# Low parts of weights by transfers that add, and Strassen's products for 14 FFN pairs of the first layer

## The chip, the cores and the metric

The kernel runs on one core of a Trainium2 chip. A core has five engines that work side by side, each through its own queue in order: TensorE (PE: matmuls; PEld is its weight loads), VectorE (DVE), ScalarE (ACT), GpSimd (POOL) and SyncE (SP, which here only issues DMA transfers). Sixteen DMA engines move data between memory and the on-chip buffer, and inside that buffer. The metric is the device time of one execution in microseconds (us).

## The reference

Two layers over 512 tokens of width 1024, in float32, then a final norm:

```
mod = c @ w_ada + b_ada                 # 6 vectors of 1024 per layer: shifts, scales, gates
h = rms_norm(x) * (1 + sc_m) + sh_m
x_lru, q_down, kv_down, k_rope, gate_a, gate_b = split(h @ w_in)
y_a = rg_lru(conv(x_lru))               # a gated linear recurrence
y_b = mla(q_down, kv_down, k_rope)      # 8 heads, causal
y = sigmoid(gate_a) * y_a + sigmoid(gate_b) * y_b
x = x + g_m * (y @ w_out)
h = rms_norm(x) * (1 + sc_f) + sh_f
gate, up = split(h @ w_ffn_in)          # 2 x 2816 columns: 22 tiles each of 128
x = x + g_f * ((silu(gate) * up) @ w_ffn_out)
```

## The kernel before

Activations lie with channels on the 128 partitions and the 512 tokens along the row, so a product with a weight of 1024 x 128 is 8 steps of 128 channels. To keep float32's precision at the speed of the shorter format fp32r, each operand is split in a high part (rounded to fp32r) and a low part (what is left), and each step is three matmuls: high x high, high x low, low x high (`mm3`). A product of 1024 x 128 with 512 tokens is thus 24 matmuls of 512 columns; it is called a unit here.

Weights come by `w_cols`: a transfer of 512 KB into one of 3 buffers `raw`, a high part `whi` by ScalarE, and a low part `wlo`, raw - whi, by VectorE (`split`), each in one of 3 buffers. For the FFN output of layer 1 alone the low part is made in another way: ScalarE writes -whi, and a transfer issued by GpSimd adds raw to it in place (`accum_op`). Such a transfer is called a transfer that adds. A raw buffer is free again when its low part is done.

A layer has an attention part (input products `w_in`: the inputs of the recurrence, the downward projections and 16 gates; then heads, recurrence, merging), a projection of 8 units (`w_out`), and the FFN. The FFN runs over 22 pairs (gate and up tile); products with the FFN output weights (`fo_block`) are done in three blocks of pairs (`FCUTS`: pairs 0 to 6, 7 to 13, 14 to 21), the first two beside the next block's pairs, the last one alone. The first pair is computed ahead of the norm (`Ahead`). Of the others the first `NPLAIN[l]` are plain: two units of 24 matmuls each. The rest are done by `fi_pair`, with Strassen's scheme in Winograd's form: gate and up tile, halves of the channels and halves of the tokens are the 2 x 2 blocks, and 7 products of 4 steps x 3 matmuls of 256 columns, 84 in all, take the place of 48 of 512. It needs sums of weight blocks (`w_quarters`: 4 sums and 5 further splits on VectorE and ScalarE) and of token halves (`token_halves`, once per layer). Layer 0 has no such pair (21 plain ones and the one ahead), layer 1 has 16.

The modulation vectors are made by VectorE: a transfer of 512 KB into one of 2 buffers `graw`, and one reduction of 128 x 1024 against c (`mod_column`, shown as CUSTOM_DVE_ANT_0 in the profile and as ISA in the order of instructions). Those of layer 1 are steps of a background list (`bg`): one step is recorded after each unit, and the rest when the list is drained.

No engine's order is written by hand. All operations are recorded with what they need; `Recorder.order` then plans a run with assumed durations, and each engine takes, at each moment of the plan, the ready operation that has the longest chain behind it. What comes out is a fixed order for each engine. The plan's figures for a transfer issued by GpSimd are `POOL_DMA` (its time on GpSimd's queue) and `POOL_LAT` (what follows until it has landed); the plan lets SyncE's transfers share one rate, and does not count GpSimd's against it. All recorded operations are issued in one line (L524 before, L530 after), so rows are told apart by the tiles that they name.

## Time and profile before

| | |
|---|---|
| time, median of 3 runs | 1330.85 us (1329.75 to 1331.48) |
| profiled execution | 1330.39 us, its span 1328.6 us |
| TensorE busy | 99% of the span |
| VectorE, ScalarE, GpSimd busy | 71%, 51%, 18% |
| granted TensorE clock, mean | 0.998 of full speed |
| DMA | 186.44 MB, mean 140 GB/s |

The span runs from the first to the last instruction of the profiled execution; its time is 1.8 us longer. Matmuls are pipelined, so what one of them costs is read from the step between the starts of two, not from its own duration. The span has layer 0's first products (to 58 us), its attention part (to 272), projection and change to the FFN (to 328), FFN (to 682); then layer 1's attention part (to 916), projection (to 977), FFN and end.

### The profile page before, as it was taken

The page shows a single profiled execution, that of the slowest core. Times are in us where ns is not written, and L with a number is a line of the kernel's source. Part 1 is how long each engine was busy: PE and PEld are TensorE (multiplying, and loading weights), DVE is VectorE, ACT ScalarE, POOL GpSimd, SP SyncE. Part 2 cuts the span into 40 slices and gives each one's busy share as a digit, 9 for nine tenths or more (in the row PEclk, how much of TensorE's full clock was granted, in tenths as well). Part 3 has the DMA queues.
Part 4 walks back from the last instruction along what each step waited for, and adds up shares of the span by engine and source line. Part 5 has one row for each costly group of instructions (what it writes and reads, how often), then busy time and mean ns, then how long its engine had stood idle before and what let it go on. Part 6 is the DMA issues. An engine that isn't in the chain of part 4 may idle for free.

```text
span 1328.6 us, 18151 instructions
## 1 busy us (share of the span) xinstructions
PE 1309.8 (99%) x6788; PEld 1119.4 (84%) x6788; DVE 945.7 (71%) x1625; ACT 676.2 (51%) x1057; POOL 235.1 (18%) x250
## 2 busy tenths in 40 slices
PE   9999999999999999999999999999999999999997
PEld 7787878888888888888888888888888999899986
DVE  7999887897755555555679886666687766667634
ACT  4597676635322222222356867855474544444532
POOL 0414534314000000000211433312400000000011
PEclk9999999999999999999999999999999999999999
DMA  8744344172655555555414231211333444544473
GB/s 291 237 121 152 117 127 143 64 229 104 220 177 181 172 209 176 183 206 172 147 59 149 94 115 64 96 48 48 106 101 109 133 118 135 155 129 134 126 157 109
DMA packets 56012, 186.44 MB, mean 140 GB/s; under 512 B 7026, under 2 KB 7282, under 8 KB 55924
## 3 DMA queue, kind: packets, MB, share of 16 engines
q1 hardware_dynamic: 52468, 173.75, 39.6%
q0 software_dynamic: 3456, 11.54, 4.7%
q8 instruction: 53, 0.87, 0.3%
q14 instruction: 35, 0.29, 0.1%
HBM read 167.44 MB, written 2.10 MB: 128 GB/s over the span
## 4 chain that ended last, share of the span: by engine, by line
PE 88%; DMA 4%; ACT 3%; DVE 2%; SPq 1%; issue 1%; POOL 0%; DVEq 0%; ACTq 0%
PE mm L524 78%; PE s L524 4%; PE o L524 2%; PE pt L524 2%; DMA raw<-in_w_in_dram 1%; DMA raw<-in_w_ada_dram 1%; SPq L524 1%; DMA graw<-in_w_ada_dram 1%; ACT whi L524 1%; ACT L524 0%; DMA raw<-in_w_ffn_in_dram 0%; DVE raw L524 0%; DMA raw<-in_w_first_dram 0%; DMA crow<-in_c_dram 0%; ACT xc L524 0%
## 5 line engine op out<-in xcount | busy, mean ns | idle before, releaser
L524 ACT ACTIVATE whi<-raw 128x1024 fp32r<-128x1024 f32 (+2 forms) x192 | 199.3, 1038 | 434.6 <-PE mm L524 318.1
L524 DVE TENSOR_TENSOR wlo<-raw,whi 128x1024 fp32r<-128x1024 f32 (+1 forms) x167 | 206.9, 1240 | 103.9 <-ACT whi L524 99.9
L524 PE MATMUL mm<-hl,whi 128*128 128x512 f32 x432 | 168.9, 391 | 0.3 <-DVE hl L524 0.3
L524 PE MATMUL mm<-hh,whi 128*128 128x512 f32 x432 | 166.2, 394 | 1.8 <-ACT ri L524 1.4
L524 PE MATMUL mm<-hh,wlo 128*128 128x512 f32 x416 | 161.8, 390 | 0.0
L524 PE MATMUL mm<-al,whi 128*128 128x512 f32 (+1 forms) x360 | 139.1, 386 | 0.0
L524 PE MATMUL mm<-ah,whi 128*128 128x512 f32 (+1 forms) x360 | 138.9, 386 | 0.0
L524 PE MATMUL mm<-ah,wlo 128*128 128x512 f32 (+1 forms) x360 | 138.5, 385 | 0.0
L524 PE MATMUL mm<-fh,whi 128*128 128x512 f32 x336 | 130.5, 389 | 0.0
L524 PE MATMUL mm<-fh,wlo 128*128 128x512 f32 x336 | 130.5, 389 | 0.0
L524 PE MATMUL mm<-fl,whi 128*128 128x512 f32 x336 | 130.4, 389 | 0.0
L524 PEld LDWEIGHTS mm<-hh,whi 128*128 128x128 f32 x432 | 80.9, 188 | 19.0 <-ACT ri L524 1.5
L524 PEld LDWEIGHTS mm<-hl,whi 128*128 128x128 f32 x432 | 81.2, 188 | 17.4 <-DVE hl L524 1.4
L524 PEld LDWEIGHTS mm<-hh,wlo 128*128 128x128 f32 x416 | 78.1, 188 | 16.0
L524 PE MATMUL mm<-xqh,wsl 128*128 128x256 f32 x320 | 90.4, 283 | 0.0
L524 PE MATMUL mm<-xql,wsh 128*128 128x256 f32 x320 | 90.4, 283 | 0.0
L524 PE MATMUL mm<-xqh,wsh 128*128 128x256 f32 x320 | 90.4, 284 | 0.0
L524 DVE CUSTOM_DVE_ANT_0 graw<-graw,cb,cols 128x1024 f32<-128x1024 f32 x64 | 83.4, 1303 | 6.5 <-DMA graw<-in_w_ada_dram 5.7
L524 POOL TENSOR_SCALAR wsa<-raw,mod 128x128 f32<-128x128 f32 x24 | 17.2, 736 | 388.6 <-PE mm L524 339.4
L524 PEld LDWEIGHTS mm<-ah,whi 128*128 128x128 f32 x360 | 67.7, 188 | 13.2
L524 PEld LDWEIGHTS mm<-ah,wlo 128*128 128x128 f32 x360 | 67.7, 188 | 13.2
L524 PEld LDWEIGHTS mm<-al,whi 128*128 128x128 f32 x360 | 67.7, 188 | 12.6
(257 smaller groups left out, 3055.7 us busy)
## 6 DMA issues: line engine op xcount, KB each, us to landing
graw<-in_w_ada_dram SPq DMA_DIRECT2D x88, 512.0 KB, 4.5
raw<-in_w_ffn_in_dram SPq DMA_DIRECT2D x88, 512.0 KB, 3.4
raw<-in_w_in_dram SPq DMA_DIRECT2D x47, 512.0 KB, 3.4
raw<-in_w_ffn_out_dram SPq DMA_DIRECT2D x32, 448.0 KB, 3.5
raw<-in_w_out_dram SPq DMA_DIRECT2D x16, 512.0 KB, 3.4
raw<-in_w_ffn_out_dram SPq DMA_DIRECT2D x16, 512.0 KB, 3.9
wlo<-raw POOLq DMA_DIRECT2D x16, 448.0 KB, 4.4
raw<-in_w_ada_dram SPq DMA_DIRECT2D x8, 512.0 KB, 4.7
```

The costliest lines, as they stand in the source:

```text
L524: o.call(*(real(v) for v in o.a), **{k: real(v) for k, v in o.k.items()})
```

## The change

Three edits. First, the low parts of more weights are made by transfers that add: all of `w_in` that goes by `x_lru` and `gate` (20 weights in layer 0, 24 in layer 1; here GpSimd writes -whi, by `tensor_scalar`), `w_out` (16) and layer 0's `w_fo` (24; in both of these ScalarE writes -whi, as layer 1's `w_fo` did already). `w_fi` and the units of `Ahead` keep the subtraction on VectorE. Second, `NPLAIN` of layer 0 goes from 21 to 7, so 14 pairs go by `fi_pair`, and the layer takes the path with `token_halves`. Third, the plan's figures for GpSimd's transfers go from 1200 and 6000 ns to 900 and 3700.

```diff
-NPLAIN = (21, 5)
+NPLAIN = (7, 5)
...
-POOL_DMA = 1200.0
-POOL_LAT = 6000.0
+HOW_IN = "gg"
+HOW_OUT = "aa"
+HOW_FI = "vv"
+HOW_FO = "aa"
+HOW_A1 = "v"
+POOL_DMA = 900.0
+POOL_LAT = 3700.0
...
+    def split_by(how, hi, lo, src):
+        if how == "v":
+            split(hi, lo, src)
+            return
+        A.activation(hi, src, AF.Copy)
+        if how == "a":
+            A.activation(lo, f(hi), AF.Copy, scale=-1.0)
+        else:
+            G.tensor_scalar(lo, f(hi), -1.0, 1.0, ALU.mult, ALU.mult)
+        G.dma_start(f(lo), src, accum_op=ALU.add)
...
-    def w_cols(src, nk=KD, raws=None, dma=False):
+    def w_cols(src, nk=KD, raws=None, how="v"):
...
-        if dma:
-            A.activation(hi[:, : nk * P], raw[:, : nk * P], AF.Copy)
-            A.activation(lo[:, : nk * P], f(hi[:, : nk * P]), AF.Copy, scale=-1.0)
-            G.dma_start(f(lo[:, : nk * P]), raw[:, : nk * P], accum_op=ALU.add)
-        else:
-            split(hi[:, : nk * P], lo[:, : nk * P], raw[:, : nk * P])
+        split_by(how, hi[:, : nk * P], lo[:, : nk * P], raw[:, : nk * P])
...
-                ps = product(w_cols(w_in[l, n]))
+                ps = product(w_cols(w_in[l, n], how=HOW_IN[l]))
...
-            ps = product(w_cols(w_in[l, off + h]))
+            ps = product(w_cols(w_in[l, off + h], how=HOW_IN[l]))
...
-            [(m, FULL) for m in range(KD)], yh, yl, lambda m: w_cols(w_out[l, m]), done_out,
+            [(m, FULL) for m in range(KD)], yh, yl, lambda m: w_cols(w_out[l, m], how=HOW_OUT[l]), done_out,
...
-                lambda m: w_cols(w_fo[l, m, :, k0 * P : (k0 + nk) * P], nk, dma=last), done,
+                lambda m: w_cols(w_fo[l, m, :, k0 * P : (k0 + nk) * P], nk, how=HOW_FO[l]), done,
```

In numbers of instructions: 14 pairs x 48 = 672 matmuls of 512 columns go, 14 x 84 = 1176 of 256 columns come; 98 subtractions of weights on VectorE go (82 of 1024 columns, 16 of 896): the 84 whose low part is now made by a transfer, and 14 because `w_quarters` subtracts one weight where a plain pair has two; GpSimd has 108 transfers that add instead of 24, and 44 negations of 1024 columns more.

Since the plan is made anew, each engine's order changes. Three places:

GpSimd's queue where layer 0's first input products end; w16 is a chain of small operations for the recurrence's parameters, 108 and 109 (137 and 138) are the high and low part of the first (second) input weight. Before:

```order
L524 TENSOR_TENSOR w16_4_71<-w16_4_71,w16_3_561 128x16
L524 TENSOR_SCALAR w16_4_71<-w16_4_71 128x16
L524 TENSOR_TENSOR w16_4_71<-w16_4_71,w16_3_561 128x16
L524 TENSOR_SCALAR w16_4_71<-w16_4_71 128x16
L524 TENSOR_TENSOR w16_4_71<-w16_4_71,w16_3_561 128x16
L524 TENSOR_SCALAR w16_4_71<-w16_4_71 128x16
L524 TENSOR_TENSOR w16_4_71<-w16_4_71,w16_3_561 128x16
```

After:

```order
L530 TENSOR_TENSOR w16_4_71<-w16_4_71,w16_3_561 128x16
L530 TENSOR_SCALAR w16_4_71<-w16_4_71 128x16
L530 TENSOR_TENSOR w16_4_71<-w16_4_71,w16_3_561 128x16
L530 TENSOR_SCALAR w16_4_71<-w16_4_71 128x16
L530 TENSOR_SCALAR wlo_109_626<-whi_108_611 128x1024
L530 TENSOR_TENSOR w16_4_71<-w16_4_71,w16_3_561 128x16
L530 DMA wlo_109_626<-raw_107_569 128x1024
L530 TENSOR_SCALAR wlo_138_649<-whi_137_630 128x1024
L530 TENSOR_SCALAR w16_4_71<-w16_4_71 128x16
L530 DMA wlo_138_649<-raw_136_589 128x1024
```

Two negations and two transfers that add stand in the middle of the chain of small operations.

TensorE's queue at the same place; mm_45 is the last of the first products, mm_110 and mm_139 are the products with those two weights. Before:

```order
L524 MATMUL mm_45_333<-hl_37_609,whi_96_591 128x512
L524 MATMUL mm_110_679<-hh_22_271,whi_108_611 128x512
L524 MATMUL mm_110_679<-hl_30_285,whi_108_611 128x512
L524 MATMUL mm_110_679<-hh_22_271,wlo_109_622 128x512
L524 MATMUL mm_110_679<-hh_23_328,whi_108_611 128x512
```

After:

```order
L530 MATMUL mm_45_333<-hl_37_609,whi_96_591 128x512
L530 MATMUL mm_110_674<-hh_22_271,whi_108_611 128x512
L530 MATMUL mm_110_674<-hl_30_285,whi_108_611 128x512
L530 MATMUL mm_139_681<-hh_22_271,whi_137_630 128x512
L530 MATMUL mm_139_681<-hl_30_285,whi_137_630 128x512
L530 MATMUL mm_110_674<-hh_22_271,wlo_109_626 128x512
L530 MATMUL mm_110_674<-hh_23_328,whi_108_611 128x512
```

Two matmuls of the second product have moved between the high parts of the first and its first matmul with a low part.

VectorE's queue at the beginning of layer 0's last FFN block; x0_73, x1_79 are residuals after a unit, xw and sacc the low part and the sum of squares made from them, ISA with graw a reduction for layer 1's modulation. Before:

```order
L524 SCALAR_TENSOR_TENSOR x0_73<-mm_1099_5512,mod0_5_3488,x0_73 128x512
L524 ISA graw_1094_5519,mod1_5_5360<-graw_1094_5519,cb_187,cols1_130 128x1024
L524 ISA mod1_5_5360 128x1
L524 TENSOR_TENSOR wlo_1119_5568<-raw_1117_5456,whi_1118_5547 128x1024
L524 SCALAR_TENSOR_TENSOR xw_1102_5575<-x0_73,mod1_1_3759,xh_1101_5563 128x512
L524 ISA graw_1095_5549,mod1_5_5360<-graw_1095_5549,cb_187,cols1_130 128x1024
L524 ISA mod1_5_5360 128x1
L524 SCALAR_TENSOR_TENSOR x1_79<-mm_1106_5551,mod0_5_3488,x1_79 128x512
L524 TENSOR_TENSOR wlo_1126_5597<-raw_1124_5495,whi_1125_5589 128x1024
L524 TENSOR_TENSOR sacc_1100_5559<-sacc_1100_5559,sq_1107_5600 128x512
L524 SCALAR_TENSOR_TENSOR xw_1109_5614<-x1_79,mod1_1_3759,xh_1108_5604 128x512
```

After:

```order
L530 SCALAR_TENSOR_TENSOR x0_73<-mm_1333_6522,mod0_5_3691,x0_73 128x512
L530 ISA graw_1302_6529,mod1_2_5920<-graw_1302_6529,cb_187,cols1_130 128x1024
L530 ISA mod1_2_5920 128x1
L530 SCALAR_TENSOR_TENSOR xw_1336_6588<-x0_73,mod1_1_3851,xh_1335_6583 128x512
L530 ISA graw_1303_6558,mod1_2_5920<-graw_1303_6558,cb_187,cols1_130 128x1024
L530 ISA mod1_2_5920 128x1
L530 SCALAR_TENSOR_TENSOR x1_79<-mm_1340_6560,mod0_5_3691,x1_79 128x512
L530 ISA graw_1304_6580,mod1_2_5920<-graw_1304_6580,cb_187,cols1_130 128x1024
L530 ISA mod1_2_5920 128x1
L530 TENSOR_TENSOR sacc_1334_6575<-sacc_1334_6575,sq_1341_6620 128x512
L530 SCALAR_TENSOR_TENSOR xw_1343_6636<-x1_79,mod1_1_3851,xh_1342_6626 128x512
```

Subtractions of weights are gone from this queue, and reductions stand in their place; up to the first operand of layer 1 (ht) 17 of them follow the first residual, where 2 did before. In the attention part of layer 1, behind that operand, there are 10, where there were none. In the FFN before that block, 14 stand in the plain pairs and 15 in the Strassen pairs, where 54 did in all between the projection and the last block.

## Rows read from the trace of the kernel before

**Rows 1.** the page, part 1: busy us, share of the span, instructions

```profile
PE 1309.8 (99%) x6788; PEld 1119.4 (84%) x6788; DVE 945.7 (71%) x1625; ACT 676.2 (51%) x1057; POOL 235.1 (18%) x250
```

**Rows 2.** stages: length, PE, PEld, DVE, ACT, POOL busy us, clock, DMA, GB/s

```profile
58.00:272.00 214.00, 207.32 (x1051) 174.91 (x1050) 188.59 (x373) 155.16 (x272) 86.43 (x80) 1.00 0.39 125
272.00:328.00 56.00, 56.00 (x256) 46.53 (x256) 47.70 (x70) 26.21 (x37) 20.09 (x22) 1.00 0.53 174
...
682.00:916.00 234.00, 233.97 (x1184) 199.24 (x1183) 181.37 (x358) 167.34 (x281) 65.82 (x63) 1.00 0.27 84
...
1032.00:1250.00 218.00, 216.96 (x1542) 204.77 (x1541) 149.59 (x254) 105.12 (x172) 14.04 (x16) 1.00 0.48 132
...
1278.00:1308.00 30.00, 30.00 (x144) 24.81 (x143) 11.51 (x31) 11.89 (x15) 4.35 (x5) 1.00 0.67 141
```

**Rows 3.** the chain that ended last, from start time, us

```profile
327.91 351.60 PE mm L524 x1550
...
688.97 3.79 PE mm L524 x16
...
1145.38 5.77 DMA raw<-in_w_ffn_in_dram
```

**Rows 4.** timeline of TensorE: start, us, operation

```profile
1138.17 0.28 PE L524 MATMUL mm<-xqh,wsl 128*128 128x256 f32 x1
...
1140.69 0.29 PE L524 MATMUL mm<-xqh,wsl 128*128 128x256 f32 x1
...
1143.32 0.39 PE L524 MATMUL mm<-ah,whi 128*128 128x512 f32 x1
...
1149.90 0.39 PE L524 MATMUL mm<-ah,wlo 128*128 128x512 f32 x1
```

**Rows 5.** groups by line and form: busy us, mean ns of one

```profile
L524 DVE TENSOR_TENSOR wlo<-raw,whi 128x1024 fp32r<-128x1024 f32 x143 | 180.8, 1265 | 99.0 <-ACT whi L524 96.0 <-PE pt L524 0.3
...
L524 DVE CUSTOM_DVE_ANT_0 graw<-graw,cb,cols 128x1024 f32<-128x1024 f32 x64 | 83.4, 1303 | 6.5 <-DMA graw<-in_w_ada_dram 5.7 <-ACT cb L524 0.4
...
L524 ACT ACTIVATE wlo<-whi 128x1024 fp32r<-128x1024 f32 x8 | 8.5, 1058 | 0.2
...
L524 POOL DMA_DIRECT2D wlo<-raw x24 | 21.0, 875 | 322.8 <-ACT wlo L524 174.0 <-ACT pq L524 74.6 <-PE mm L524 60.2
...
L524 POOL TENSOR_SCALAR sc<-sc,sm 128x512 f32<-128x512 f32 x16 | 14.9, 929 | 73.7 <-DVE sm L524 55.5 <-PE o L524 12.7 <-issue 5.4
...
L524 POOL TENSOR_SCALAR sc<-sc,sm 128x128 f32<-128x128 f32 x16 | 11.3, 709 | 0.0
```

**Rows 6.** the tile wlo: its transfers

```profile
DMA to landing us min/median/max: 4.2/4.6/7.9
```

**Rows 7.** timeline of ScalarE at the first input weight

```profile
56.05 1.06 ACT L524 ACTIVATE whi<-raw 128x1024 fp32r<-128x1024 f32 x1 [0.71 <-DMA raw<-in_w_in_dram]
```

**Rows 8.** timeline of TensorE there

```profile
61.60 0.39 PE L524 MATMUL mm<-hh,whi 128*128 128x512 f32 x1
```

**Rows 9.** timeline of GpSimd there

```profile
58.53 0.57 POOL L524 TENSOR_SCALAR w<-w 128x16 f32<-128x16 f32 x1
```

**Rows 10.** timeline of VectorE and GpSimd at 96 us

```profile
96.37 1.57 POOL L524 TENSOR_TENSOR ri<-ri,xc 128x512 f32<-128x512 f32 x1 [7.61 <-ACT ri L524]
...
96.70 2.32 DVE L524 TENSOR_TENSOR wlo<-raw,whi 128x1024 fp32r<-128x1024 f32 x1
```

**Rows 11.** the page, parts 3 and 6: DMA queues; issues, median to landing

```profile
q1 hardware_dynamic: 52468, 173.75, 39.6%
q0 software_dynamic: 3456, 11.54, 4.7%
...
graw<-in_w_ada_dram SPq DMA_DIRECT2D x88, 512.0 KB, 4.5
```

**Rows 12.** timeline of VectorE at layer 0's last FFN block

```profile
638.30 0.75 DVE L524 SCALAR_TENSOR_TENSOR x<-mm,mod,x 128x512 f32<-128x512 f32 x1 [1.58 <-PE mm L524]
...
683.37 2.08 DVE L524 SCALAR_TENSOR_TENSOR ht<-x,mod,rs 128x512 f32<-128x512 f32 x3 [1.91 <-ACT rs L524]
```

More of the change, by code (lines that the diff above doesn't have):

```diff
@@ L887, in w_quarters @@
         h, l_ = hl_tiles()
-        split(h, l_, raws[0])
+        split_by(HOW_A1, h, l_, raws[0])
         res["A11"], res["A12"] = (h[:, lo_], l_[:, lo_]), (h[:, hi_], l_[:, hi_])
@@ L1418, in w_fi_cols @@
         def w_fi_cols(m):
-            return w_cols(w_fi[l, m // 2 + (m % 2) * NF])
+            return w_cols(w_fi[l, m // 2 + (m % 2) * NF], how=HOW_FI[l])
         def residual(m, cs, ps):
```

## The prediction

> **What bounds the kernel now.** I read the busy times first: TensorE is busy in 99% of the span, VectorE in 71%, ScalarE in 51%, GpSimd in 18% [rows 1]. Then the busy time by stage [rows 2]: only the attention part of layer 0 (58 to 272 us) leaves TensorE visibly idle, 214.00 - 207.32 = 6.7 us, and there VectorE is at 188.59 / 214 = 88%. In the same part of layer 1 VectorE is at 181.37 / 234 = 78% and TensorE is idle 0.03 us. In the FFN stages TensorE is full; with Strassen (1032 to 1250 us) VectorE is at 69% and TensorE idle about 1 us. The chain of work that ended last says the same [rows 3]: one piece of 351.60 us is TensorE alone (layer 0's FFN), and in Strassen's stage the chain leaves TensorE where a weight load comes late, 5.77 us at 1145.38. So time can come from two places: fewer or shorter matmuls, and layer 0's 6.7 us of waits behind a full VectorE.
>
> **Strassen for 14 pairs.** Where nothing waits, 29 steps of 512 columns take 1149.90 - 1143.32 = 6.58 us, 0.2269 us each, and 21 steps of 256 columns take 1140.69 - 1138.17 = 2.52 us, 0.120 us each [rows 4]. A plain pair is 2 x 8 x 3 = 48 matmuls of 512 columns, 10.89 us; a Strassen pair is 7 products of 4 x 3 = 84 matmuls of 256 columns, 10.08 us. The saving is 0.81 us a pair, **-11.3 us** for 14.
>
> The price is VectorE work. Layer 1 does the same with VectorE at 69% [rows 2], with one stall of about 1.2 us at 1153 where an FFN load came late [rows 3]. Layer 0 adds reductions for layer 1's modulation (1.303 us each [rows 5]), 15 during its Strassen pairs in the new order: some 20 us over about 217, so 79% instead of 69%. That still fits. Bounds of the stalls: 0, and one such 1.2 us per block of FFN output, 3 in all, plus as much again: 5. I take **+1.5**.
>
> **Low parts by transfers that add.** A subtraction on VectorE, 1.265 us, goes for 44 attention input weights (20 in layer 0, 24 in layer 1), 16 of the projection and 24 of layer 0's FFN output. In layer 0's attention that is 20 x 1.265 = 25 us of 188.59, so VectorE falls to about 76%, where layer 1 shows no idle TensorE at 78%. Of the 6.7 us I take **-5** (bounds 0 and -6.7): some waits are for loads, which this edit does not help.
>
> What replaces it is slower in latency. For the input weights GpSimd negates the high part: the trace has no such operation at 1024 columns; 128 columns take 0.709 us in the mean, 512 take 0.929 [rows 5], so some 1.2 by that slope, and 0.7 to 2.4 as bounds. For the projection and FFN output ScalarE does it in 1.058 us; in the projection it is busy for 26.21 of 56 us [rows 2], so 8 more are covered. Then GpSimd issues a transfer: 0.875 us on its queue [rows 5], landing 4.2 / 4.6 / 7.9 us (least, median, most) after the issue [rows 6]. So a low part is ready some 6 us after its high part instead of 1.3.
>
> Where it is not covered: the first weight of layer 0. Its high part starts at 56.05 [rows 7], and TensorE comes to it at 61.60 [rows 8], so before, 4 us lay between. In the new order its negation stands behind four polynomial steps on GpSimd, the fourth of which ends at 58.53 + 0.57 = 59.1 [rows 9]. With 1.2 for the negation, some 0.3 for the step between, and 4.6 to land, it is there at 65.2. TensorE has four matmuls with high parts first, 61.60 + 0.9 = 62.5, and then waits: **+2.8** (2.3 with the shortest landing, 6 with the longest). Later weights have other TensorE work ahead of them and the weights' buffers hold three, so I count none.
>
> A rule against this edit: GpSimd's reads and VectorE's operations with two inputs from SBUF hold each other up. The rows show it: a subtraction that takes 1.265 us in the mean took 2.32 at 96.70, beside a GpSimd operation at 96.37 [rows 10]. The Trainium skill, "SBUF — State Buffer", Who interferes with whom, says that the second to issue is blocked until the first is done; the trace agrees. My sum takes the mean durations, in which such waits are; if each of the 44 negations costs a further 1.1 us (2.32 - 1.265), that is 48 us spread over both engines, and the rival below prices it.
>
> **The transfers' own load.** Queue q1 moved 173.75 MB in 39.6% of 1328.6 us, so 512 KB (0.524 MB) take 1.59 us of all 16 engines. Queue q0, the transfers that add, took 4.7% for 11.54 MB: 2.84 us for 512 KB [rows 11]. In layer 0's attention 20 of them add 57 us to a share of 0.39 over 214 us: 0.66. That is covered. In the projection (272 to 328 us, share 0.53 [rows 2]) up to 8 add 23 us to 30 of 56: 0.94. Lateness there between 0 and 4; I take **+1**.
>
> The worst place is the end of layer 0. The reductions that Strassen pushes out of the FFN stage move into its last block: 17 stand between the first residual and layer 1's first operand where 2 stood, on the in-order queue of VectorE. In the trace these two points are 638.30 and 683.37 [rows 12]; the block itself begins one unit of 24 x 0.227 = 5.45 us earlier, so 50.5 us hold all of it. DMA work in that time: 17 reductions x 1.59 = 27, some 8.5 weight loads x 1.59 = 13.5, 5 transfers that add x 2.84 = 14: 55 us. Besides, the reductions have two buffers: each pair costs 1.30 for a reduction, 4.5 to land [rows 11] and some 0.2 between, 6.0 us, 51 us for 8.5 pairs with no queueing, and if each pair waits behind one load or transfer (2.2 on average), 70. So layer 1's operand comes 0 to 19 us late; I take 9, nearer to the DMA's own sum. TensorE reads it at 688.97 [rows 3], where it can be there at about 685: 4 us are covered. **+5** (bounds 0 and 15).
>
> Layer 1's attention loses 24 x 1.265 = 30 us of VectorE work and gets 10 reductions more, 13 us. TensorE was not idle there: **0** (bounds -1 and +5, for late low parts).
>
> Sum: -11.3 + 1.5 - 5 + 2.8 + 1 + 5 + 0 = **-6.0**. The profiled execution took 1330.39 us, so 1324.4; the median of the runs is 0.46 above it: 1324.8, which I round to **1324.5**.
>
> **The rivals.**
> *All is covered.* The DMA queues take the extra load in gaps, the last block is not late, TensorE keeps full in layer 0. For: layer 1's last block (1278 to 1308 us) runs such transfers at a DMA share of 0.67 with TensorE full [rows 2]. Then -11.3 - 6.7 + 2.8 + 1 = -14: about 1316, down to 1312 without stalls.
> *GpSimd and VectorE block each other.* Of the 48 us one in six to eight reaches TensorE, 6 to 8 us: 1331, no change that a measurement of this kernel can tell (within 0.2%, 2.7 us). For: the subtraction at 96.70. Against: GpSimd is busy for 86.43 of 214 us there, so most operations meet nothing.
> *The DMA queues bound the last block: slower.* Loads wait behind reductions on the in-order issue queue, so the block's own weights come late too. A unit needs 3 x 1.59 + 2.84 = 7.6 us of DMA against 5.45 of TensorE: 8 x 2.15 = 17 us in place of my 5: 1336.5. It turns slower than before once lateness at this place passes 11 us. For: two reductions stand in each unit. Against: three weight buffers are filled ahead.
> *The change does not do what it says.* The new order has 84 matmuls of 256 columns for each of 14 pairs; excluded.
>
> **How the numbers follow.** Forecast (1319 to 1329 with its bounds) 50%; all covered 22%; blocking 13%; DMA bound 12%; other 3%. Faster by over 0.2% (below 1328.2): most of the forecast's 50, the 22 and a little of the blocking, 0.74. Within 0.2%: 0.14. Slower: 0.12. The range leaves out the half of each outer case: 1312 to 1333.
>
> **What would show it.** The FFN stage of layer 0 shorter by about 10 us with 256-column steps of 0.120; a TensorE wait of about 3 us near 62 us; idle TensorE in the rest of layer 0's attention under 3 us; a wait near the start of layer 1 behind a reduction on VectorE that waits for its load. Wrong would be: no wait there and a time near 1316, or FFN units of the last block paced above 5.45 us and a time above 1333; also TensorE waits spread over both attention parts behind low parts in flight.

## The result and the profile after

The changed kernel takes 1376.92 us (median of 4 runs, 1374.7 to 1382.45); the kernel before took 1331.16 us beside it (4 runs). The ratio is 1.0343 [1.0311, 1.0375]: it is 46 us slower, where 6 us less were forecast. The profiled execution took 1374.7 us, its span is 1372.8 us.

The page of the changed kernel (parts 1, 3 and 6; columns as in [rows 1] and [rows 11]):

```profile
PE 1320.4 (96%) x7292; PEld 1146.9 (84%) x7292; DVE 967.0 (70%) x1747; ACT 767.9 (56%) x1207; POOL 346.4 (25%) x378
...
q1 hardware_dynamic: 52468, 173.75, 37.3%
q0 software_dynamic: 15552, 54.53, 21.3%
...
graw<-in_w_ada_dram SPq DMA_DIRECT2D x88, 512.0 KB, 4.8
...
wlo<-raw POOLq DMA_DIRECT2D x76, 512.0 KB, 5.2
```

TensorE's share fell from 99% to 96% [rows 1], and no other engine has become full: VectorE, the busiest of them, is at 70%. The transfers that add went from 4.7% to 21.3% of the DMA engines' span; 54.53 MB in 292 us is 2.81 us for 512 KB, the 2.84 us of the prediction. A reduction's load lands 4.8 us after its issue instead of 4.5.

By stage (columns as in [rows 2]; the last three rows are short stretches inside the first and the fourth):

```profile
58.00:288.30 230.30, 212.87 (x1036) 178.69 (x1035) 171.00 (x346) 168.53 (x282) 118.76 (x123) 0.96 0.62 163
288.30:337.50 49.20, 46.98 (x204) 38.58 (x203) 33.49 (x50) 23.56 (x30) 15.81 (x23) 0.97 0.80 232
...
351.30:644.00 292.70, 290.84 (x1832) 263.81 (x1831) 224.21 (x371) 141.13 (x220) 15.64 (x18) 1.00 0.57 174
644.00:705.20 61.20, 51.56 (x216) 41.85 (x215) 37.20 (x54) 25.62 (x32) 23.92 (x28) 0.92 0.89 263
...
719.00:965.00 246.00, 237.31 (x1171) 200.49 (x1171) 173.53 (x353) 170.61 (x283) 116.11 (x113) 0.98 0.59 153
...
65.30:68.20 2.90, 2.90 (x7) 2.32 (x8) 2.90 (x5) 2.81 (x5) 2.48 (x6) 0.50 0.99 192
...
697.60:703.10 5.50, 5.50 (x13) 4.39 (x14) 4.78 (x8) 2.74 (x4) 5.50 (x8) 0.50 0.77 266
703.20:705.20 2.00, 2.00 (x10) 1.64 (x9) 0.80 (x1) 0.00 (x0) 1.84 (x3) 1.00 0.90 352
```

Before, attention and projection of layer 0, its last FFN block, and the attention of layer 1:

```profile
58.00:269.90 211.90, 205.22 (x1039) 172.94 (x1038) 186.66 (x370) 155.03 (x271) 86.43 (x80) 1.00 0.38 122
269.90:315.00 45.10, 45.10 (x204) 37.55 (x203) 40.00 (x56) 18.70 (x25) 19.88 (x22) 1.00 0.61 198
...
627.70:676.10 48.40, 48.40 (x215) 40.11 (x214) 33.83 (x40) 19.70 (x26) 15.74 (x22) 1.00 0.42 137
...
688.70:920.40 231.70, 231.67 (x1171) 197.36 (x1171) 178.77 (x355) 163.52 (x276) 65.82 (x63) 1.00 0.28 87
```

Three of them now let TensorE wait where before it was idle little or not at all: layer 0's attention for 17.4 us (6.7 before [rows 2]), the last FFN block of layer 0 for 9.6 us (0 before), layer 1's attention for 8.7 us (0.03 before). VectorE has become emptier, as meant: 74% in layer 0's attention instead of 88%, 71% in layer 1's instead of 78%. And the DMA share is 0.62 and 0.59 there (0.39 and 0.27 before), 0.80 in the projection (0.61), 0.89 in the last block (0.42).

What TensorE waited for over the whole span, the first four entries (us in total, times, longest):

```profile
PE mm L530 <- DMA wlo<-raw: 14.9, 4, 7.7
PE pt L530 <- POOL sc L530: 6.1, 1, 6.1
PE s L530 <- DVE kl L530: 3.8, 1, 3.8
PE o L530 <- ACT ph L530: 3.7, 1, 3.7
```

The low parts by transfers lead the list, with 4 waits: one at the start of layer 0's attention, one in its projection, two in its last FFN block. The other entries are waits for engines that were late themselves.

The stages of all profiled executions, from the first matmul of one stage to the first of the next in TensorE's timeline. First row: us of before; then differences to it. "Attention 0" begins with the first product; that comes up to 2.9 us sooner or later from run to run, as the first loads arrive, which is the column "start".

| kernel | start | attention 0 | projection 0 | to FFN 0 | FFN 0, 21 pairs | last block | to layer 1 | attention 1 | rest | span |
|---|---|---|---|---|---|---|---|---|---|---|
| before | 17.9 | 251.9 | 45.2 | 12.7 | 299.9 | 48.5 | 12.7 | 231.7 | 408.1 | 1328.6 |
| changed | -0.8 | +19.2 | +4.1 | +1.3 | -7.5 | +12.8 | +1.2 | +14.3 | -0.4 | +44.2 |
| transfers | -0.6 | +19.4 | +2.8 | +1.5 | -0.1 | +1.7 | +0.2 | +6.6 | +0.7 | +32.3 |
| strassen | -0.1 | -0.9 | 0.0 | 0.0 | -10.5 | -0.5 | +8.2 | +8.1 | +0.2 | +4.6 |
| thin | +0.9 | +7.2 | 0.0 | +0.3 | -10.6 | +0.1 | +7.9 | +8.1 | -1.1 | +12.8 |
| thin_a | -0.5 | +5.6 | 0.0 | +0.4 | -10.8 | +0.6 | +8.6 | +3.6 | -1.4 | +6.1 |
| in_v | +1.2 | +1.2 | +4.9 | +0.9 | -6.3 | +8.9 | +1.5 | +5.4 | +1.6 | +19.3 |
| strassen_bg | -0.7 | +2.0 | 0.0 | 0.0 | -10.1 | -0.3 | 0.0 | +2.3 | -0.8 | -7.6 |
| after_bg | +1.6 | +22.6 | +4.1 | +1.5 | +4.0 | -0.5 | +0.5 | +7.7 | -0.5 | +40.8 |
| fo_bg | +2.9 | +2.1 | 0.0 | 0.0 | +2.0 | -0.5 | +0.5 | +0.7 | +0.7 | +8.2 |
| fo_bg_raw4 | -0.6 | +5.4 | 0.0 | 0.0 | -2.3 | -0.4 | 0.0 | +2.4 | -0.8 | +3.7 |
| load_only | +2.5 | +6.2 | 0.0 | 0.0 | -2.3 | -0.3 | 0.0 | +0.7 | +2.5 | +9.4 |
| after_raw4 | +2.5 | +9.7 | +6.1 | 0.0 | -6.6 | +9.9 | +2.9 | +12.8 | -0.9 | +36.4 |
| plan_old | -0.3 | +12.5 | +0.3 | +0.9 | -8.1 | +0.1 | +10.8 | +12.7 | -0.4 | +28.5 |
| after_all | +0.6 | +9.9 | +1.5 | 0.0 | -4.5 | +0.6 | 0.0 | +9.2 | -0.9 | +16.6 |

Attention 0 has differed by up to 7 us (-0.9 to +6.2) between kernels that have no new work in it (strassen, strassen_bg, fo_bg, load_only): the order is planned anew for each, so less than that is not read there. And each row is a single execution: strassen_bg's eight took 1320.97 to 1330.93 us. One execution of the kernel plan_dma took 4350.63 us, its profiled one: its profile is not used, and its time is the median of its other runs.

**Two places in the timeline.** First the wait that was forecast near 62 us (start, us, engine, operation; in brackets the idle time before and what ended it):

```profile
57.97 1.07 ACT L530 ACTIVATE whi<-raw 128x1024 fp32r<-128x1024 f32 x1 [1.88 <-DMA raw<-in_w_in_dram]
...
58.93 1.18 POOL L530 TENSOR_SCALAR wlo<-whi 128x1024 fp32r<-128x1024 f32 x1
...
60.45 1.05 POOL L530 DMA_DIRECT2D wlo<-raw  x1
...
65.22 0.79 PE L530 MATMUL mm<-hh,wlo 128*128 128x512 f32 x1 [3.06 <-DMA wlo<-raw]
```

The negation follows its high part at once, takes 1.18 us (1.2 forecast), the transfer is issued at 60.45, and TensorE waits 3.06 us for it, until 65.22 (65.2 forecast). That the time fits to 0.1 us is in part luck: the high part began 1.9 us later than before (57.97, 56.05 in [rows 7]) and so ended at 59.04, just when GpSimd's four polynomial steps, from which the forecast counted, were done as well.

Then the longest wait of all, in the last FFN block of layer 0:

```profile
676.05 1.29 DVE L530 CUSTOM_DVE_ANT_0 graw<-graw,cb,bsc 128x1024 f32<-128x1024 f32 x1 [6.18 <-DMA graw<-in_w_ada_dram]
...
677.38 2.80 SPq L530 DMA_DIRECT2D graw<-in_w_ada_dram  x2
680.28 0.37 SPq L530 DMA_DIRECT2D raw<-in_w_in_dram  x1
...
680.52 0.63 ACT L530 ACTIVATE sq<-x 128x512 f32<-128x512 f32 x1 [7.05 <-DVE x L530]
...
682.75 1.06 ACT L530 ACTIVATE wlo<-whi 128x1024 fp32r<-128x1024 f32 x1
...
685.29 2.49 POOL L530 TENSOR_SCALAR wsa<-raw,mod 128x128 f32<-128x128 f32 x4 [10.56 <-DMA raw<-in_w_in_dram]
687.76 2.99 POOL L530 TENSOR_SCALAR wsb<-raw,mod 128x128 f32<-128x128 f32 x3
690.70 0.87 POOL L530 DMA_DIRECT2D wlo<-raw  x1
...
697.53 0.80 PE L530 MATMUL mm<-ah,wlo 128*128 128x512 f32 x1 [7.69 <-DMA wlo<-raw]
```

ScalarE has written -whi of a weight at 682.75 + 1.06 = 683.81. GpSimd could issue its transfer then, but the transfer stands behind seven small operations for layer 1's first products in GpSimd's in-order queue, and the first of these has waited 10.56 us for a weight load that SyncE issued only at 680.28. So the transfer goes out at 690.70, 6.9 us late, and TensorE waits 7.69 us, until 697.53. Both ends of this go back to one late load: VectorE had stood idle for 6.18 us until 676.05, before a reduction whose load had not landed. Behind that reduction stood a residual, for which ScalarE waited 7.05 us until 680.52 before it came to this weight; and when the reduction had freed its buffer, SyncE issued two loads for reductions (677.38) and only then, in its in-order queue, the weight load at 680.28.

### The profile page after: what moved, and what is told of

It reads as the page before. It is cut to its first block, busy times and chain, and to the rows that moved or that the text cites. A ratio compares the mean times of both kernels' runs of the same rounds, so it can differ in the third digit from the quotient of the medians.

```text
span 1372.8 us, 19779 instructions
## 1 busy us (share of the span) xinstructions
PE 1320.4 (96%) x7292; PEld 1146.9 (84%) x7292; DVE 967.0 (70%) x1747; ACT 767.9 (56%) x1207; POOL 346.4 (25%) x378
## 3 DMA queue, kind: packets, MB, share of 16 engines
q0 software_dynamic: 15552, 54.53, 21.3%
## 4 chain that ended last, share of the span: by engine, by line
PE 63%; issue 12%; DMA 10%; DVE 8%; POOL 5%; ACT 1%; SPq 1%; DVEq 0%; POOLq 0%; ACTq 0%
PE mm L530 55%; DMA wlo<-raw 3%; DMA graw<-in_w_ada_dram 3%; PE s L530 3%; PE o L530 2%; PE pt L530 2%; DMA raw<-in_w_ffn_in_dram 1%; DVE graw L530 1%; POOL wlo L530 1%; DMA raw<-in_w_ffn_out_dram 1%; POOL wsa L530 1%; DVE t L530 1%; DVE xc L530 1%; SPq L530 1%; POOL sc L530 1%
## 5 line engine op out<-in xcount | busy, mean ns | idle before, releaser
L530 ACT ACTIVATE whi<-raw 128x1024 fp32r<-128x1024 f32 (+3 forms) x178 | 184.1, 1035 | 271.4 <-PE mm L530 191.5
L530 POOL DMA_DIRECT2D wlo<-raw x108 | 95.4, 886 | 690.4 <-ACT wlo L530 486.2
L530 PE MATMUL mm<-xqh,wsh 128*128 128x256 f32 x600 | 170.0, 284 | 1.6 <-DVE pq L530 1.5
L530 PE MATMUL mm<-xql,wsh 128*128 128x256 f32 x600 | 169.5, 283 | 0.0
L530 PE MATMUL mm<-xqh,whi 128*128 128x256 f32 (+1 forms) x432 | 142.8, 331 | 0.2 <-ACT pq L530 0.2
L530 PE MATMUL mm<-xqh,wlo 128*128 128x256 f32 (+1 forms) x432 | 142.3, 330 | 0.0
L530 PE MATMUL mm<-xql,whi 128*128 128x256 f32 (+1 forms) x432 | 142.0, 330 | 0.0
L530 PEld LDWEIGHTS mm<-xqh,wsh 128*128 128x128 f32 x600 | 114.6, 192 | 3.1 <-DVE pq L530 2.8
L530 PEld LDWEIGHTS mm<-xql,wsh 128*128 128x128 f32 x600 | 115.0, 192 | 0.5
L530 PEld LDWEIGHTS mm<-xqh,wsl 128*128 128x128 f32 x600 | 114.9, 192 | 0.0
```

Of the source, the lines that this page charges most:

```text
L530: o.call(*(real(v) for v in o.a), **{k: real(v) for k, v in o.k.items()})
```

## The experiments

**transfers**: the change with plain pairs, `NPLAIN = (21, 5)`.

> The change without Strassen in layer 0: its first layer's FFN goes back to 21 plain pairs, all low parts stay with the transfers that add. Against the kernel before, the changed kernel loses 18.5 us in layer 0's attention, 14.3 us in layer 1's, 5.4 us in the first projection and its change to the FFN, 14 us in the last FFN block of layer 0 and its norm, and gains 7.5 us in that FFN. Theory 1 (the transfers that add cause the losses by their load and lateness): both attention parts and the projection stay long, 18.5 + 14.3 + 5.4 = 38 us over before, the last block is a little late: 1369 to 1375 us. Theory 2 (Strassen, which pushes the modulation reductions into the last block and layer 1's attention, causes those two): layer 1's attention and the last block come back, 18.5 + 5.4 = 24 us remain: about 1355 us. Theory 3 (the transfers cost little by themselves): 1331 to 1338 us.

Measured: 1363.89 us, ratio 1.025 [1.0222, 1.0278]. The low parts by transfers, with the plan's new figures, cost 32 us by themselves: both attention parts and the projection stay long (+19.4, +6.6, +2.8), so theory 3 falls. But layer 1's attention loses only 6.6 of the 14.3 us and the last block 1.7 of 12.8: the time is 5 us below theory 1's range, and theory 2 has a share.

**strassen**: the kernel before with `NPLAIN = (7, 5)`, and nothing else.

> Strassen for 14 pairs of layer 0 alone: the kernel before with that one number changed, all other low parts by VectorE and the plan's old figures. 14 x 0.81 = 11.3 us less TensorE work. Theory 1 (the transfers cause the losses): attention parts as before, the last block may be some us late because the reductions still move into it: 1320 to 1327 us. Theory 2 (the displaced reductions cause the last block's and layer 1's losses, 28 us): about 1345 us. Theory 3 (VectorE becomes full in the Strassen pairs without the relief by transfers): the FFN does not get shorter, 1328 to 1335 us.

Measured: 1337.3 us, ratio 1.0039 [1.0025, 1.0053]. The FFN is 10.5 us shorter, as worked out, though VectorE keeps all subtractions. 16 us are lost behind it, more than theory 1 had and less than theory 2. The stages to layer 1 and of its attention in this run:

```profile
664.00:685.00 21.00, 16.26 (x66) 13.20 (x64) 16.75 (x27) 7.55 (x13) 3.57 (x3) 0.84 0.69 218
685.00:925.00 240.00, 234.72 (x1169) 199.21 (x1170) 198.14 (x377) 165.50 (x280) 70.24 (x63) 0.99 0.32 100
```

And its timeline at the end of layer 0, of VectorE and then TensorE:

```profile
667.33 1.48 DVE L524 CUSTOM_DVE_ANT_0 graw<-graw,cb,cols 128x1024 f32<-128x1024 f32 x1
...
668.74 1.27 DVE L524 CUSTOM_DVE_ANT_0 graw<-graw,cb,cols 128x1024 f32<-128x1024 f32 x1
...
669.95 0.74 DVE L524 SCALAR_TENSOR_TENSOR x<-mm,mod,x 128x512 f32<-128x512 f32 x1
...
671.74 0.68 DVE L524 TENSOR_TENSOR sacc<-sacc,sq 128x512 f32<-128x512 f32 x1
...
672.48 0.80 PE L524 MATMUL o<-ones,sacc 128*128 128x1 f32 x3 [3.61 <-DVE sacc L524]
```

VectorE runs without a gap here: the reductions have their data, but stand ahead of the residual (669.95) and of the sum of squares (671.74) that TensorE waits for 3.61 us, at 672.48. So it is VectorE's queue that is too long at this place, not DMA.

**thin**: the changed kernel in its own order, with each transfer that adds cut to 16 partitions when it is issued:

```diff
+                if o.eng == "POOL" and o.dur == POOL_DMA:
+                    args = [v[:16] for v in args]
```

> The changed kernel with the same order of every engine, but each of the 108 transfers that add moves 16 of 128 partitions (64 of 512 KB), so most of each low part stays -whi and the output is not the reference's. The issue on GpSimd's queue, the negations, the waits and the fixed part of the latency stay; the load on the DMA engines goes from 21.3% of the span to under 3%. Theory 1a (the load of the transfers delays the weights' and reductions' loads): most of the loss goes, 1320 to 1335 us. Theory 1b (the longer way of a low part through GpSimd's in-order queue and the fixed latency of a transfer): most stays, 1360 to 1372 us. Theory 2 (the reductions' place in the order): attention and last block stay late, 1355 us or more.

Measured: 1345.45 us, ratio 1.0109 [1.0074, 1.0144], 10 us above theory 1a's range. 31 us of the 46 go with the size of the transfers, though every instruction stays in its place: theory 1a for most of it. The load did not fall as far as expected. An eighth of the bytes still takes a third of the DMA engines' time, 7.3% of the span and not under 3%:

```profile
q0 software_dynamic: 3456, 6.82, 7.3%
```

The last block, the projection and 12 of 19 us of attention 0 come back; what is left, 12.8 us of span, is Strassen's pattern (+7.9 and +8.1, less what the FFN gains) and 7.2 us in attention 0. A transfer lands sooner, too. The summary for the low parts' tile in thin:

```profile
DMA to landing us min/median/max: 2.9/3.1/6.8
```

The same of the changed kernel:

```profile
DMA to landing us min/median/max: 4.2/5.0/10.9
```

so low parts are ready and raw buffers are free 2 us earlier as well, and thin doesn't part load from lateness and held buffers.

**in_v**: the change with `HOW_IN = "vv"`.

> The changed kernel with the attention input weights' low parts back on VectorE by subtraction (44 weights); the projection and FFN output keep the transfers, Strassen stays. Theory 1 (the input transfers and their negations cause both attention parts' loss, 33 us): 1344 us or less. Theory 2 (the reductions cause layer 1's part): only layer 0's 18.5 us go, about 1358 us. Theory 3 (VectorE's relief was worth something there): layer 0's attention is about as long as before the change, layer 1's is longer since VectorE has 24 subtractions and 10 reductions more: 1350 to 1360 us.

Measured: 1349.78 us, ratio 1.0145 [1.0108, 1.0181]. That is 6 us above theory 1's bound, at the lower edge of theory 3's range. Attention 0 is back within 1.2 us of before, attention 1 at +5.4: the transfers of the attention inputs, with their negations, cost 18 and 9 us there, beyond anything that VectorE's relief bought.

**strassen_bg**: strassen with the reductions recorded in the pairs, at the end of `fi_pair`:

```diff
+            bg(2)
```

> Strassen alone was 4.6 us longer in its span than before: its FFN was 10.5 us shorter, but the change to layer 1 8.2 us and layer 1's attention 8.1 us longer. Here each Strassen pair of layer 0 also records two steps of the background list, as a plain pair does, so the reductions for layer 1 stand in the FFN as before (22 between the first residuals of the first and the second block, 18 and 20 before that, 2 in the last block) and none in layer 1's attention. Theory A (the displaced reductions cause both losses): both vanish, 16 us less than Strassen alone, about 1321 us. Theory B (VectorE, 84% busy in Strassen's FFN, cannot take 24 reductions more, 31 us of 288, 95%): the losses vanish but the FFN stage gains less than 5 us instead of 10.5: 1326 to 1332 us. Theory C (the two losses have another cause, such as a new order that is poor by itself): 1337 us as before.

Measured: 1325.79 us (8 runs), ratio 0.9946 [0.9924, 0.9968]: faster than both kernels. Theory A: to layer 1 0.0, attention 1 +2.3, and the FFN keeps 10.1 of its 10.5 us. Theory B falls:

```profile
329.00:619.00 290.00, 289.84 (x1831) 263.60 (x1831) 265.74 (x435) 125.68 (x202) 0.00 (x0) 1.00 0.58 194
```

VectorE is busy for 265.74 of 290 us, 92%, and TensorE is idle for 0.16 us. So 92% of VectorE did not hold up TensorE in this stage.

**after_bg**: the changed kernel with the same line.

> The changed kernel with the same two background steps recorded in each Strassen pair. If displaced reductions and transfers add up: the last block of layer 0 comes back from 12.8 us over before to about 2, layer 1's attention from 14.3 to about 6.5, as in the run with transfers alone, and the FFN stays near 7 us shorter; layer 0's attention and projection keep their 23 us: 1355 us. If the reductions' loads and the transfers crowd the DMA queues in the FFN instead, the FFN loses its gain: 1362 us.

Measured: 1370.74 us, ratio 1.0277 [1.0255, 1.0299]. The last block (-0.5) and attention 1 (+7.7) come back as expected, but the FFN goes from -7.5 to +4.0: the second outcome in kind, though 9 us above its 1362. With the transfers, the FFN loses its gain when the reductions are put back (DMA share 0.68 there, 0.57 in the change).

**thin_a**: thin, with `HOW_IN = "aa"` (ScalarE negates).

> The kernel with thin transfers (16 of 128 partitions, so the output is not the reference's) once more, but ScalarE instead of GpSimd writes -whi of the attention input weights (the order is planned anew). With thin transfers layer 0's attention stayed 8.1 us longer than before, the DMA load being gone. Theory Q (the negations in GpSimd's in-order queue, which wait there for late high parts while the recurrence's operations stand behind them): layer 0's attention comes within 2 us of before. Theory L (the latency of a transfer, 3 us at least after its issue): it stays 5 us or more longer.

Measured: 1336.83 us (one run). Attention 0 stays at +5.6, by the expectation theory L; attention 1 goes from +8.1 to +3.6, which speaks for Q there. Neither alone, and attention 0's 5.6 us are within what planning anew moves. But the two runs show something else. Layer 0's attention in thin, where GpSimd negates:

```profile
58.00:278.00 220.00, 208.42 (x1041) 175.08 (x1039) 172.37 (x347) 168.52 (x282) 119.74 (x124) 0.98 0.47 125
```

And in thin_a, where ScalarE does:

```profile
58.00:275.00 217.00, 206.52 (x1037) 174.43 (x1036) 156.81 (x345) 182.88 (x299) 92.63 (x103) 0.98 0.47 126
```

With nearly the same number of instructions VectorE is busy for 172.37 us beside GpSimd's negations and for 156.81 without them: they make VectorE's own operations longer, by 15.6 us in this stage.

**fo_bg**: strassen_bg with layer 0's FFN output by transfers (the change with `bg(2)`, `HOW_IN = "vv"`, `HOW_OUT = "vv"`; the plan's new figures).

> Only Strassen, with the two background steps in each pair, and layer 0's FFN output by transfers that add, with the plan's new figures; attention inputs and projection by VectorE as before. Theory A (VectorE relief is worth something where VectorE is fullest, in the FFN with Strassen and reductions): at least 2 us faster than Strassen with background steps alone. Theory B (the transfers' load delays the weights' and reductions' loads there too): some 3 us slower than it or more.

Measured: 1338.54 us (10 runs), ratio 1.0047 [1.0029, 1.0065], 12.7 us more than strassen_bg: theory B, though the plan's figures differ between the two runs as well. The FFN, the only stage with new transfers beside the last block, is 12.1 us longer. VectorE has 17 us less work there and still TensorE waits. The FFN stage of fo_bg:

```profile
332.00:634.00 302.00, 294.13 (x1831) 265.36 (x1830) 248.94 (x418) 141.11 (x221) 15.74 (x18) 0.99 0.69 208
```

What VectorE's sums of weight blocks (ws) waited for there, in fo_bg:

```profile
DVE ws L530 <- DMA raw<-in_w_ffn_in_dram: 16.3, 8, 4.4
```

And in strassen_bg:

```profile
DVE ws L524 <- DMA raw<-in_w_ffn_in_dram: 1.5, 3, 0.6
```

16.3 us of waiting for loads with the transfers, 1.5 us without.

**fo_bg_raw4** and **load_only** part the two ways in which a transfer can make loads late. The first is fo_bg with `NRAW = 4` and `NU = 71`; the second is strassen_bg with an idle transfer beside each FFN output weight of layer 0 (and `NU = 71`):

```diff
+                    G.dma_start(dummy[:, :nk * P], cb[:, :nk * P], accum_op=ALU.add)
```

> Strassen with background steps and layer 0's FFN output by transfers that add lost in its FFN stage what Strassen alone had gained: 12 us more than without the transfers (DMA share 0.69 instead of 0.58). Here it has four raw buffers instead of three (one of the 72 small tiles less, to make room). Theory B1 (a raw buffer is held until its transfer has landed, some 5 us longer than by a subtraction, so the next load is issued late): the FFN stage comes back by 6 us or more, to about 1331 us. Theory B2 (the transfers' load on the DMA engines makes the loads themselves slow): it comes back by less than 3 us, 1335 us or more.

Measured: 1339.7 us, ratio 1.0069 [1.0043, 1.0094]; the time does not come back (fo_bg 1338.54), so theory B2 by the time. In the profiled execution the FFN comes back by 4.3 of 12.1 us, but that is the fastest of six (1334.17 us), while fo_bg's is an ordinary one: a share of held buffers is not shown here.

> Strassen with background steps, all low parts of layer 0's FFN output by VectorE as in that fast version, and beside each of these weights an idle transfer that adds, of the same size, from a constant into a tile that nobody reads: it loads the DMA engines as the real ones do, but holds no raw buffer and nothing waits for it. Theory B2 (load): the FFN stage gets longer by 8 us or more against the version without, about 1335 us. Theory B1 (buffers): by less than 3 us, about 1327 us.

Measured: 1341.38 us, ratio 1.0091 [1.0064, 1.0118]; 15.6 us more than strassen_bg (fo_bg: 12.7 more). In the profiled execution the FFN is 7.8 us longer, nearly the 8 of theory B2; the rest lies before layer 0's FFN and behind layer 1's attention, where there are no idle transfers. Its FFN stage:

```profile
329.00:630.00 301.00, 295.27 (x1833) 267.01 (x1832) 267.78 (x439) 131.20 (x211) 15.38 (x18) 0.99 0.70 215
```

So load that holds no raw buffer and that no other engine waits for costs the FFN 7.8 us, where the real transfers cost 12.1; what makes up the difference is not shown. The load acts through SyncE's loads. For those of reductions VectorE waited in this stage, in load_only:

```profile
DVE graw L524 <- DMA graw<-in_w_ada_dram: 19.0, 10, 3.9
```

And in strassen_bg:

```profile
DVE graw L524 <- DMA graw<-in_w_ada_dram: 8.0, 9, 1.8
```

The Trainium skill, "DMA: Bandwidth & Descriptors", Issuing engines are not separate DMA queues, says that transfers run on the same 16 engines and interleave, whichever engine issued them; load_only agrees with it: beside GpSimd's idle transfers VectorE waits 19.0 us instead of 8.0 for SyncE's loads.

**after_raw4**: the changed kernel with `NRAW = 4`, `NU = 71`.

> The changed kernel with four raw buffers instead of three (one small tile of 72 less). Theory B1 (held buffers delay the loads, and what stands behind them in SyncE's in-order queue, the reductions' loads among it): most of the 31 us that thin transfers gave back come back here too, 1350 us or less. Theory B2 (load of the DMA engines): little changes, 1368 to 1380 us.

Measured: 1365.76 us, ratio 1.0279 [1.0243, 1.0314]: 11 us less than the change, a little below theory B2's bound, and far from B1's 27. So held buffers have a share, about a quarter if nothing else in the new order helped. One wait in attention 0 shows how. The chain of work there in the changed kernel (start, us):

```profile
113.97 6.55 DMA wlo<-raw
120.58 0.33 SPq L530
...
121.01 4.42 DMA graw<-in_w_ada_dram
```

What stood behind it, of VectorE and TensorE:

```profile
125.56 2.99 DVE L530 CUSTOM_DVE_ANT_0 graw<-graw,cb,cols 128x1024 f32<-128x1024 f32 x1 [3.48 <-DMA graw<-in_w_ada_dram]
...
129.22 0.50 PE L530 MATMUL s<-xch,lwh 128*128 128x512 f32 x1 [3.79 <-DVE kl L530]
```

A raw buffer is held until a transfer that adds has landed, at 120.5. Only then SyncE issues the next weight load, and behind it in its queue the load for a reduction. The reduction waits 3.48 us for it, kl stands behind the reduction, and TensorE waits 3.79 us for kl, its longest wait in this stage. With four buffers VectorE waits 2.8 us for such loads in attention 0 instead of 7.2; over the whole span it is still 51.3 us, against 52.2 in the change.

**plan_old**: the changed kernel with the plan's old figures, 1200 and 6000 ns.

> The changed kernel with the plan's old figures for a transfer that adds (1200 ns on the queue and 6000 ns to land, where measured are 886 ns and 5.0 us in the median) instead of 900 and 3700. Theory P (the plan counts a low part ready 1.3 us too early, so products stand too early in TensorE's order and wait): waits for low parts go, 1360 us or less. Rival (waits are set by load and buffers that the plan does not see): within 5 us of the changed kernel, 1372 to 1382 us.

Measured: 1363.98 us, ratio 1.0281 [1.0228, 1.0335]: 13 us less than the change, not as far down as theory P asked, and below the rival's range. The projection and the last block lose their waits (+0.3, +0.1); the reductions then show in the step to layer 1 (+10.8). The third edit, the new figures, cost 13 us by itself.

**plan_dma**: the changed kernel with a plan that counts these transfers against the DMA rate:

```diff
-                    end += POOL_LAT
+                    dma_free = max(dma_free, end) + 2840.0 * o.a[0].shape[1] / 1024
+                    end = dma_free + 600.0
```

> The changed kernel with a plan that counts each transfer that adds against the DMA rate, 2.84 us for 512 KB as read from the trace of before, and lets it land 0.6 us after; all else as changed. Theory P2 (the loss comes from orders made for loads and low parts that arrive sooner than they do): at least 20 us come back, 1357 us or less, and more than the old figures gave (1364 us). Theory L (the load itself delays what the engines need, whatever the order): 1362 us or more.

Measured: 1354.27 us, ratio 1.0164 [1.0117, 1.0211]: 22.6 us less than the change. Theory P2: half of the loss goes when only the plan changes, so it comes from orders made for data that arrives sooner than it does.

**after_all**: plan_dma, `bg(2)` in the pairs, and four raw buffers.

> The changed kernel with all causes mended that the runs named: the plan counts the transfers, two background steps are recorded in each Strassen pair, four raw buffers (71 small tiles). If these causes are what made the loss and only a part of the load itself is left: 1335 to 1348 us. If the load itself is the greater part of it: above 1355 us. If the transfers are worth their relief of VectorE once they are planned for: below 1325.8 us, the time of Strassen with background steps and no new transfers.

Measured: 1347.4 us, ratio 1.013 [1.0076, 1.0185]. 29.5 of the 46 us are mended, at the upper end of what was expected if the named causes are the loss; 21.6 us above strassen_bg are left, about a third of them in attention 0 (+9.9 against +2.0), the rest mostly in attention 1 (+9.2 against +2.3) and the FFN (-4.5 against -10.1). Once planned for, the transfers are still not worth VectorE's relief.

## Why the prediction was wrong

**Strassen's gain was right.** 11.3 less 1.5 us were forecast for the pairs; alone the FFN gained 10.5, and in the change 7.5. (The stall in layer 1 that the forecast put at about 1.2 us is 1.04 us in the row of that stage [rows 2].)

**The step that failed: "That is covered", for the transfers' load.** The shares themselves were near or too high: 0.66 worked out for attention 0 and 0.62 measured, 0.94 for the projection with the change to the FFN and 0.72 measured (288.3 to 351.3 us). The step from a share below 1 to a cost of nothing (+1 in the projection) was wrong: these two stages became 19.2 and 5.4 us longer. What the share leaves out: engines follow an order fixed beforehand, in which every load has its time. A load that comes later stops VectorE at a reduction, and what stands behind it. For reductions VectorE waited (waits of VectorE over the span). Changed:

```profile
DVE graw L530 <- DMA graw<-in_w_ada_dram: 52.2, 30, 6.2
```

Before:

```profile
DVE graw L524 <- DMA graw<-in_w_ada_dram: 8.5, 16, 1.6
```

52.2 us instead of 8.5 (23.9 in thin). 22.4 of them lie in layer 0's last block and the step behind it, 7.2 in its attention. That the size of the transfers is the cause is shown by thin (-31 us with no instruction moved), and that their load alone does such harm, by load_only (7.8 us in the FFN with a load that no other engine waits for), though only for that stage and in another kernel; that the plan's ignorance of the load is half of the damage, by plan_dma (-22.6); that buffers held longer add to it, by after_raw4 (-11) and the wait at 129.22. These shares overlap and do not add up.

**"Of the 6.7 us I take -5" had the wrong sign.** Attention 0 became 19.2 us longer. VectorE at 88% was taken for the cause of TensorE's idle time there, because layer 1 at 78% had none. strassen_bg holds TensorE full at 92%. in_v, with the subtractions back, has the same attention 0 as before. And a lower share did not help: in thin_a VectorE is at 72% there, and TensorE is idle for 10.5 us. So VectorE's share is not shown to be the cause of the 6.7 us. By the list of waits of before, those 6.7 us are eight single waits, none over 1.4 us, 4.2 us of them for ScalarE; why ScalarE is late there is open.

**The first low part was right** in its wait, 3.06 us at 65.22 with +2.8 forecast, in part by luck, and its cost was more than its wait (see the last section). That "later weights have other TensorE work ahead of them" was wrong in the projection and the last block: the list of waits has three more, the longest 7.7 us.

**The end of layer 0 and layer 1's attention: right in kind, too small, and in part for another reason.** +5 and 0 were forecast; Strassen alone lost 8.2 and 8.1, the change 14.0 and 14.3. The displaced reductions are the cause, shown by strassen_bg, where one line that puts them back takes both losses away but for 2.3 us. In Strassen alone the limit is VectorE's queue, and not DMA, which the prediction took; with the transfers' load on top it is DMA, and what the prediction didn't look at: GpSimd's queue, where a transfer stood behind sums that waited for a load. The 10 reductions in layer 1's attention were costed at nothing since VectorE loses 30 us of work and gains 13: the same error of the mean share.

**The third edit had no term in the sum.** It cost 13 us.

**The rivals.** "The DMA queues bound the last block" came nearest: its 17 us for that place are near the 14.0 that the block and the step behind it took, but it was thought of for that place alone, and the same mechanism cost more in the two attention parts. "GpSimd and VectorE block each other" was true as well, and the forecast's sum had it at nothing beyond the mean durations: thin and thin_a show 15.6 us of it on VectorE in attention 0. It reaches TensorE in the wait at 129.22: the reduction there took 2.99 us (1.303 in the mean before [rows 5]) beside a GpSimd operation of 1.49 us at 125.97. (The mean of a subtraction does not show it, 1268 ns in place of 1265 [rows 5]: those that are left stand mostly in the FFN, where GpSimd is busy for 15.64 of 292.70 us.) What it costs in time is not measured by itself: thin_a, a single run, is 8.6 us faster than thin, but it also takes the negations out of GpSimd's queue. The sign "TensorE waits spread over both attention parts behind low parts in flight" came true by half: the waits are spread, but only one of them, at 65.22, is directly for a low part.

**Left open**: how the 21.6 us of after_all above strassen_bg divide; and attention 0's 5 to 7 us in thin and thin_a, which may be a transfer's latency, what is left of the load, in thin GpSimd's negations, or only the new order; and how the loss divides between load, held buffers and blocking.

## What to carry to other kernels

A mean share of the DMA engines or of an engine below 1 covers nothing by itself where engines follow fixed orders: ask for each load how late it may come, and what stands behind the instruction that waits for it. Work that went from a busy engine to DMA paid here in load, in buffers held longer and in operations of GpSimd that slowed VectorE; before it goes, check that the busy engine holds anybody up. And where a loop hands out background work, a new branch in it must hand it out too: here one line turned 6 us lost (strassen) into 5 us gained (strassen_bg).

## What the runs showed of the hardware

A wait of TensorE cost more than its length here. After the wait of 7.69 us the granted clock was 0.50, the lower of its two levels, from 697.6 to 703.1: 13 matmuls fall into 5.5 us there, and 10 into the 2.0 us behind it at 1.00 (the last two rows of the stages above). At the full clock 13 take 13 x 0.227 = 3.0 us, so this stretch lost 2.5 us beyond the wait. The mean granted clock fell from 0.998 to 0.982 over the span. The wait of 3.06 us until 65.22 was followed by such a stretch too (the row at 65.30); the prediction had priced each wait at its length alone. In the attention and projection of layer 0, its last block and the attention of layer 1 TensorE is busy for 7.7, 1.9, 3.2 and 5.6 us longer than before with the same matmuls (counts within 3), at a mean granted clock of 0.96, 0.97, 0.92 and 0.98 in place of 1.00. That is 18 of the 50 us by which these stages grew.

Transfers that add took the DMA engines longer here than their bytes say: 512 KB took 2.81 to 2.84 us of all 16 engines, a load of that size 1.59, and cut to an eighth of the bytes the 108 transfers still took 7.3% of 1341.4 us, 0.91 us each. And in layer 0's attention VectorE was busy for 172.37 us with GpSimd's negations and for 156.81 with ScalarE's (thin and thin_a).
